# ifftshift of an 8192 x 8192 matrix in DRAM-to-DRAM copies: seven small copies go, half a block opens and closes the scalar queue, and the right half trails the left by 384 rows

## The chip, the core and the metric

The kernel runs on one core of one Trainium2 chip. It uses no compute engine for its work: two engines, SyncE and ScalarE, each issue copies from DRAM to DRAM into a queue of their own, and 16 DMA engines of the core serve both queues. The metric is the device time of one execution in microseconds (us).

## The reference

```python
def setup_inputs():
    return {
        "x": np.random.randn(8192, 8192).astype(np.float32),
    }

def reference(x: np.ndarray) -> np.ndarray:
    return np.fft.ifftshift(x)
```

Both sides are even, so the shift swaps the four quadrants: output row r, column c comes from input row (r + 4096) mod 8192, column (c + 4096) mod 8192. Nothing is computed. 268.4 MB are read once and written once.

## The kernel before

An output row is cut into a left half (columns 0 to 4095) and a right half (columns 4096 to 8191), 16 KiB each. The left halves of all 8192 rows go through the queue of SyncE (SP, `nc.sync`), the right halves through the queue of ScalarE (ACT, `nc.scalar`). The helper `copy` (line 26) issues one copy; it works out the source address from the destination row and column and uses the same pattern `dims` on both sides.

A **block** is 256 rows (`rows = ENGINES * per`, 16 times 16). Its pattern, `back` (line 45), has three levels: 16 neighbouring rows, then 16 steps of 16 rows *upwards*, then the 16 KiB of a row half. The outermost level is 16 wide, and the 16 DMA engines take one row of each group of 16. So a block gives every engine 16 packets of 16 KiB on that queue. I call one such set of 16 packets, one on each engine, a **round**: 16 row halves, 256 KiB, and a distance of 512 KiB in memory to the next round. A queue has 32 blocks, or 512 rounds.

Both queues go from the bottom of the matrix to its top. The loop of line 47 takes four blocks at a time. The left half takes them in the order 3, 2, 1, 0; the right half (line 50) takes block `(n + 2) % 4`, so 1, 0, 3, 2. While the left half is in block 3 or 2 of four, the right half is 512 rows above it, and while the left half is in 1 or 0, the right half is 512 rows below it.

Before the loop, lines 36 to 42 treat the first 16 rows of the right half on their own. Seven **small copies** on the scalar queue take them in four column strips of 4 KiB a row. Three strips are cut in two, after 14, 9 and 4 rows:

```python
    for n, k in enumerate((14, 9, 4)):
        col = hc + n * strip
        copy(nc.scalar, start + rows - ENGINES, col, [[C, k], [1, strip]])
        copy(nc.scalar, start + rows - ENGINES + k, col, [[C, ENGINES - k], [1, strip]])
```

A copy of k rows occupies k engines, so the engines get between one and seven small packets before the long copies. The block that those rows belong to is then issued with 15 steps in place of 16 (`rest`, line 46).

The order of the work is set by the two queues and by semaphores that the framework assigns in turn. There are eight of them for copies, and a copy whose semaphore was used before waits on its issuing engine until the earlier copy has landed. In the long run each queue has four blocks under way: a copy waits for the one four places ahead of it on its own queue. At the start it is different. The seven small copies and the first sync block take all eight semaphores. The second sync block therefore waits for the first sync block to land, and the first four long scalar copies wait for small copies.

Of the kernel before, what the change touches and what calls it, by code (L numbers as in the profile page):

```python
# [1 line left out]

# [4 lines left out]


ENGINES = 16


@with_exitstack
def kernel(
    ctx: ExitStack,
    tc: tile.TileContext,
    x: bass.AP,
    out: bass.AP,
):
    nc = tc.nc
    R, C = x.shape  # L20
    hr = R // 2
    hc = C // 2
    per = 16
    rows = ENGINES * per

    def copy(queue, row, col, dims):

        src = (row + hr) % R * C + (col + hc) % C
        queue.dma_start(
            out=bass.AP(out.tensor, out.offset + row * C + col, dims),  # L30
            in_=bass.AP(x.tensor, x.offset + src, dims),
        )

    start = R - 3 * rows
    strip = hc // 4
    for n, k in enumerate((14, 9, 4)):
        col = hc + n * strip
        copy(nc.scalar, start + rows - ENGINES, col, [[C, k], [1, strip]])  # L40
        copy(nc.scalar, start + rows - ENGINES + k, col, [[C, ENGINES - k], [1, strip]])
    copy(nc.scalar, start + rows - ENGINES, hc + 3 * strip, [[C, ENGINES], [1, strip]])


    back = [[C, ENGINES], [-ENGINES * C, per], [1, hc]]
    rest = [[C, ENGINES], [-ENGINES * C, per - 1], [1, hc]]
    for first in range(R - 4 * rows, -1, -4 * rows):
        for n in (3, 2, 1, 0):
            copy(nc.sync, first + n * rows + rows - ENGINES, 0, back)
            right = first + (n + 2) % 4 * rows  # L50
            if right == start:
                copy(nc.scalar, right + rows - 2 * ENGINES, hc, rest)
            else:
                copy(nc.scalar, right + rows - ENGINES, hc, back)


# [1 line left out]
_INS = ['x']  # L58
_OUTS = [((8192, 8192), 'float32')]


# [23 lines left out]
```

## Time and profile before

| | |
|---|---|
| median of 3 runs | 810.01 us (808.99 to 810.94) |
| profiled execution, its own time | 812.71 us |
| its span in the profile | 810.9 us |
| moved | 268.44 MB read, 268.44 MB written |
| mean rate | 331 GB/s each way, 662 GB/s read and written together |
| copies | 32 blocks on SP; 7 small ones, one of 15 steps and 31 blocks on ACT |
| share of the 16 DMA engines' time | SP's queue (q1) 49.7%, ACT's queue (q10) 49.6% |

The span is counted from the first instruction; 1.81 us of the execution's own time lie outside it. The four memsets on POOL are constants of the framework, 0.2 us in all. No compute engine has any other work, so the profile's parts on engines are nearly empty, and what is to be read is the part on DMA: the rate in slices of time, the packets, and when copies are issued and land. In answers about stretches of time each line gives the stretch, its length, POOL's busy time, a clock that is of no interest here, the mean busy share of the 16 DMA engines and the rate in GB/s. Packets are counted whole in these, so a short stretch can show a share a little over 1.

### The profile page before, as it was taken

What the parts mean: (1) busy time and instruction counts of PE and PEld (TensorE: products, weight loads), DVE (VectorE), ACT (ScalarE), POOL (GpSimd) and SP (SyncE); (2) the same over time, 40 slices, a digit from 0 to 9 for tenths busy, and PEclk for the clock granted to TensorE, in tenths of its full rate; (3) what the DMA queues carried; (4) which work ended last, traced back from release to release, by engine and by line L of the source; (5) the groups of instructions that cost most, each with busy time, mean ns of one, the idle gap of its engine ahead of it and who ended that gap; (6) DMA issues with size and microseconds to landing.
All of it is one profiled execution on the core that took longest, in us unless ns stands there. A gap on an engine that the chain in (4) does not pass through costs nothing. (4 is left out here: it accounts for less than half of the span.)

```text
span 810.9 us, 116 instructions
## 1 busy us (share of the span) xinstructions
POOL 0.2 (0%) x4
## 2 busy tenths in 40 slices
POOL 0000000000000000000000000000000000000000
DMA  9999999999999999999999999999999999999998
GB/s 302 328 335 329 334 333 331 331 335 330 326 331 329 331 335 330 332 332 337 335 336 333 333 337 330 334 335 331 336 331 333 335 334 335 333 330 336 333 338 296
DMA packets 17520, 268.44 MB, mean 331 GB/s; under 512 B 1088, under 2 KB 1088, under 8 KB 1152
## 3 DMA queue, kind: packets, MB, share of 16 engines
q1 hardware_dynamic: 8704, 134.22, 49.7%
q10 hardware_dynamic: 8816, 134.22, 49.6%
HBM read 268.44 MB, written 268.44 MB: 662 GB/s over the span
## 5 line engine op out<-in xcount | busy, mean ns | idle before, releaser
L69 POOL MEMSET const-bfloat16-1.0<- 128x1 bf16 x1 | 0.1, 102 | 0.0
L69 POOL MEMSET const-uint8-127<- 128x1 uint8 x1 | 0.1, 102 | 0.0
L69 POOL MEMSET const-float32-0.0<- 128x1 f32 x1 | 0.1, 99 | 0.2 <-issue 0.2
L69 POOL MEMSET const-float32-1.0<- 128x1 f32 x1 | 0.1, 99 | 0.0
## 6 DMA issues: line engine op xcount, KB each, us to landing
out_dram<-in_x_dram SPq DMA_DIRECT2D x32, 4096.0 KB, 100.9
out_dram<-in_x_dram ACTq DMA_DIRECT2D x31, 4096.0 KB
out_dram<-in_x_dram ACTq DMA_DIRECT2D x1, 3840.0 KB
out_dram<-in_x_dram ACTq DMA_DIRECT2D x1, 64.0 KB, 10.8
out_dram<-in_x_dram ACTq DMA_DIRECT2D x1, 56.0 KB
out_dram<-in_x_dram ACTq DMA_DIRECT2D x1, 48.0 KB
out_dram<-in_x_dram ACTq DMA_DIRECT2D x1, 36.0 KB
out_dram<-in_x_dram ACTq DMA_DIRECT2D x1, 28.0 KB
```

What stands on the lines that cost most here:

```text
L69: nc = _bacc.Bacc("TRN2", target_bir_lowering=False, num_devices=1)
```

## The change

The seven small copies and the 15-step copy go. The scalar queue now begins with half a block (8 steps, 128 rows), goes on with 31 whole blocks, and ends with another half. Its blocks therefore lie half a block off those of the sync queue. The scalar queue begins 384 rows above the bottom and goes straight upwards, wrapping around at the top, so the right half is written 384 rows further back than the left one throughout, where it was alternately 512 rows above and 512 below. Both orders of issue stay as they were otherwise, with four copies of each queue under way; since there are no small copies that take semaphores, all of the first four copies of each queue are issued without a wait.

```diff
-    start = R - 3 * rows
-    strip = hc // 4
-    for n, k in enumerate((14, 9, 4)):
-        col = hc + n * strip
-        copy(nc.scalar, start + rows - ENGINES, col, [[C, k], [1, strip]])
-        copy(nc.scalar, start + rows - ENGINES + k, col, [[C, ENGINES - k], [1, strip]])
-    copy(nc.scalar, start + rows - ENGINES, hc + 3 * strip, [[C, ENGINES], [1, strip]])
 
+    def back(queue, below, col, steps):
+        last = (below - 1) % R + 1 - ENGINES
+        copy(queue, last, col, [[C, ENGINES], [-ENGINES * C, steps], [1, hc]])
 
-    back = [[C, ENGINES], [-ENGINES * C, per], [1, hc]]
-    rest = [[C, ENGINES], [-ENGINES * C, per - 1], [1, hc]]
-    for first in range(R - 4 * rows, -1, -4 * rows):
-        for n in (3, 2, 1, 0):
-            copy(nc.sync, first + n * rows + rows - ENGINES, 0, back)
-            right = first + (n + 2) % 4 * rows
-            if right == start:
-                copy(nc.scalar, right + rows - 2 * ENGINES, hc, rest)
-            else:
-                copy(nc.scalar, right + rows - ENGINES, hc, back)
+    half = per // 2
+    start = R - rows - half * ENGINES
+    back(nc.scalar, start, hc, half)
+    below = start - half * ENGINES
+    for left in range(R, 0, -rows):
+        back(nc.sync, left, 0, per)
+        back(nc.scalar, below, hc, per if left > rows else half)
+        below -= rows
```

## The prediction

> **What bounds the kernel now.** I read the page's slices first, then the DMA queues, then the waits of the sync queue, then the rate in stretches of time that I chose from the landing times.
>
> The page and its DMA part:
>
> ```profile
> DMA  9999999999999999999999999999999999999998
> GB/s 302 328 335 329 334 333 331 331 335 330 326 331 329 331 335 330 332 332 337 335 336 333 333 337 330 334 335 331 336 331 333 335 334 335 333 330 336 333 338 296
> DMA packets 17520, 268.44 MB, mean 331 GB/s; under 512 B 1088, under 2 KB 1088, under 8 KB 1152
> q1 hardware_dynamic: 8704, 134.22, 49.7%
> q10 hardware_dynamic: 8816, 134.22, 49.6%
> ```
>
> The 16 DMA engines are busy in every slice, and the two queues' packets fill 99.3% of their time. So nothing waits to be issued for long; the time is the number of packets on an engine times the length of a packet. An engine has 1024 packets of 16 KiB. In the trace's packet records these last 786 ns on average, but a third of them last 608 to 611 ns and one in seven over 1000 ns. The floor of 611 ns would be 16 engines x 16,384 B / 611 ns = 429 GB/s; the rest is packets that get in each other's way in the memory. **The length of a packet is what a change must move.** Only the first and the last slice are low.
>
> The waits of the sync queue:
>
> ```profile
> SPq L29 <- DMA out_dram<-in_x_dram: 686.8, 28, 28.4
> ```
>
> 28 of 32 sync blocks waited for an older block to land. With three more blocks queued behind it (25.2 us each) that costs nothing, except for the first such wait, at the head. The head and the tail in stretches:
>
> ```profile
> 0.00:2.00 2.00, 0.20 (x4) 1.00 0.00 0
> 2.00:5.00 3.00, 0.00 (x0) 1.00 0.97 350
> 5.00:7.00 2.00, 0.00 (x0) 1.00 1.07 373
> 7.00:16.00 9.00, 0.00 (x0) 1.00 1.00 321
> ...
> 18.00:20.00 2.00, 0.00 (x0) 1.00 1.08 352
> 20.00:22.00 2.00, 0.00 (x0) 1.00 0.90 270
> 22.00:30.00 8.00, 0.00 (x0) 1.00 1.01 338
> 30.00:805.00 775.00, 0.00 (x0) 1.00 1.00 333
> 805.00:808.00 3.00, 0.00 (x0) 1.00 1.01 339
> 808.00:810.00 2.00, 0.00 (x0) 1.00 0.28 98
> ```
>
> Until about 13 us SP is almost alone (the small copies are a few packets), from 18 to 22 us ACT is alone (SP's second block waited for its first, landed at 19.25 us), and from 805 us ACT is alone again. One queue alone gets 321 to 373 GB/s, both together 333: **a second stream adds no rate and, at this distance, takes none**. Only the dip at 20 to 22 us shows engines idle.
>
> Last, a sync block from one landing to the next, in eighths (two rounds each):
>
> ```profile
> 379.40:382.53 3.13, 0.00 (x0) 1.00 1.04 351
> 382.53:385.66 3.13, 0.00 (x0) 1.00 0.97 340
> 385.66:388.78 3.12, 0.00 (x0) 1.00 0.97 326
> 388.78:391.91 3.13, 0.00 (x0) 1.00 0.99 330
> 391.91:395.04 3.13, 0.00 (x0) 1.00 1.04 345
> 395.04:398.17 3.13, 0.00 (x0) 1.00 0.98 325
> 398.17:401.29 3.12, 0.00 (x0) 1.00 1.00 326
> 401.29:404.42 3.13, 0.00 (x0) 1.00 0.98 330
> ```
>
> The means of the eighths over 26 such blocks are 339, 343, 326, 327 and 338, 331, 327, 328 GB/s (standard error 2.5). The rate depends on where in memory the streams stand, and repeats about every half block, 8 rounds or 4 MiB. That is a sign of conflicts by address.
>
> **The change part by part.**
>
> *Small copies out.* 64 packets of 4 KiB last 159 ns each at the floor, 64 x 159 / 16 = 0.64 us of every engine's time, and 64 closing packets of 9 ns in place of none make 0.04 us. They become 16 packets of 16 KiB, 16 x 786 / 16 = 0.79 us. Sum +0.11 us. ACT spends 0.57 to 1.42 us on each issue, from 0.73 to 6.5 us, while SP's first block keeps the engines full, so ACT's issue time and the 10.8 us to the landing of the last small copy are covered and their end is worth nothing. The row says that 4 KiB in 159 ns is as fast as 16 KiB in 611.
>
> The Trainium skill's page "DMA: Bandwidth & Descriptors", section "Bandwidth", has it otherwise: transfers under 64 KB are descriptor-dominated, 64 KB in 0.95 us. By it, as an estimate, seven small copies of about 0.95 us would cost 6.6 us where bulk takes 0.8, and the change would end at 804. The trace speaks against this: they run beside another queue's packets.
>
> *Waits at the head.* SP's second to fourth and ACT's first four blocks no longer wait. The dip goes: 2 us x (333 - 270) / 333 = 0.4 us gained. At most the 321 GB/s of 7 to 16 us rises to 333 as well, 0.3 us more; at least, eight issues in a row make a dip of their own and nothing is gained. I take -0.4, since the dip is the one place with idle engines. The start stays: the first packet comes at 2.18 us, behind SP's first issue (0.73 to 1.38 us).
>
> *Tail.* SP's blocks now lead ACT's by what they gain at the start. In the packet records ACT's first packet comes 2.9 us after its issue, behind four packets that each engine had taken from SP. So I expect a lead of 4 to 5.5 rounds, as now (4.4 to 5.9), and ACT alone for the last 4.5 us, as now (SP's last packet ends at 805.2, ACT's at 809.7). Cost 0, with +-0.9 for the engines' ends, which now spread from 808.3 to 809.7.
>
> *The half-block phase.* A copy's closing packet takes its queue's turn on each engine. The records show it: two packets of one queue in a row come some 18 times per block on 16 engines, on either queue, at the other's boundaries. So SP's lead drops by one round when an SP block ends and rises when an ACT block ends. Now the low lead lasts from an SP landing to the next ACT landing, 8.5 of 25.2 us; with the half block it lasts 8 rounds longer, some 21 us. Over 26 blocks the low-lead stretch ran at 338.5 GB/s and the other at 329.2. Most of this is the address pattern above: set against the same place half a block later, the low lead is ahead by 1, 11 and -1 GB/s in its three eighths (the third counts for 0.7), +4 +- 2.5. Ends: nothing, or +4 GB/s over another half block, +0.65% of 806 us, -5.2 us. I take nothing, since the parity of the half block in memory explains the difference as well.
>
> *The distance.* 512 rows, above or below, become 384 above. Without the lead that is 32 rounds either way before and 24 after: the same multiple of 8 rounds, so the half-block pattern should stay, but 4 MiB of relative position are new. The old two distances differ by just 1024 rows, 32 MiB, so that their equal rates (block means 331.6 to 333.1 by place in the group of four) say nothing of 24. Bounds: the better and the worse stretch. 338.5 throughout is 806 x (1 - 332.3 / 338.5) = -14.8 us; the worst slice of the page, 326, is +15.6 us. I take zero, because one stream alone is no faster than two.
>
> *Sum.* 0.1 - 0.4 + 0 + 0 + 0 = -0.3 us, against the profiled execution's 812.71 us (span 810.9 and 1.81 outside): 812.4. That execution lies 2.7 us above the median; against 810.01 the forecast is 809.7.
>
> **The rivals.**
>
> *Slower: the new distance collides.* One mechanism: at 24 rounds left and right packets meet in the same part of memory more often. For it: the rate does depend on address, by 327 to 343 GB/s within a block. Against: two streams lose nothing against one. Price: the second stretch's 329.2 throughout is 806 x (332.3 / 329.2 - 1) = +7.6, so 817.5; 326 is 825.5. It decides from 0.2%, a mean under 331.6 GB/s.
>
> *Faster: the low lead is worth its 4 GB/s*, 804.5; 802.3 if the whole difference of the stretches swaps with their lengths ((16.7 x 338.5 + 8.5 x 329.2) / 25.2 = 335.4). Against: three eighths, two of them with no difference.
>
> *Engines in step.* The small packets, one to seven on an engine, set the engines apart. Without them they may run in step for longer. In the records the only rounds in step, the first four, ran mostly at the floor of 611 ns until the first small packet at 5.03 us. At 393 GB/s (3 to 5 us by the stretches) for 15 us more this gains 15 x (393 - 333) / 393 = 2.3 us, 807.5. Against: from 7 to 16 us the engines were within 0.5 us of their mean and got 321.
>
> The Trainium skill's same page, section "Latency and other measured facts", says that streams in lock-step at a power-of-two row pitch lose up to half the rate and that 4 KiB of padding restores it. By it engines in step would be slower, and as an estimate 12 MiB is no better a distance than 16. The first rounds here speak against harm from being in step, and no run here shows another pitch.
>
> **How the numbers follow.** Rate as before, head and tail alone: 809.7, own range 807.5 to 811.8, chance 0.42. Slower by the distance, 812 to 826: 0.33. Faster, by the lead or in step or a luckier distance, 799 to 808: 0.25. Faster and slower by less than 0.2% (808.4 to 811.6, about what measurement tells from no change) are the same: of the first case 0.20 falls there, 0.12 below and 0.10 above. Faster 0.37, same 0.20, slower 0.43. Leaving out a tenth at each end gives 801 to 821.
>
> **What would show it.** Right: no stretch before 30 us with a share near 0.90 but the first 2 us; both queues' shares within 0.2 of 49.7 and 49.6; slices at 331 to 335; SP done 4 to 5 us before the end, low lead for 20 us of 25. Wrong: slices shifted as a whole, 327 and lower (the distance) or 336 and higher (the lead), or a first slice near 330 (in step), or one queue far ahead and a tail of more than 8 us.

## The result and the profile after

The kernel after takes 814.52 us (median of 19 runs, 809.67 to 819.71), the kernel before beside it 811.07 (808.99 to 812.49). The ratio is 1.0046, 95% interval 1.0030 to 1.0062: slower by about half a per cent, by more than the 0.2% that I called the same. Its runs also lie further apart: their standard deviation is 2.8 us, that of the kernel before 0.9. The profiled execution of after took 816.82 us, 815.0 of them span; it is one of the slower ones.

The page after, parts on slices and DMA queues:

```profile
DMA  8999999999999999999999999999999999999998
GB/s 303 334 332 334 330 335 334 336 330 333 335 330 326 333 329 335 338 322 337 333 329 326 332 324 326 330 335 327 331 328 328 328 333 335 333 330 334 330 328 289
DMA packets 17424, 268.44 MB, mean 329 GB/s; under 512 B 1040, under 2 KB 1040, under 8 KB 1040
...
q10 hardware_dynamic: 8720, 134.22, 49.6%
q1 hardware_dynamic: 8704, 134.22, 49.4%
```

The small packets are gone (1040 closing packets are left of 1152 packets under 8 KB). The two queues' shares add up to 99.0%, where they were 99.3. The first half of the slices is as it was; from the 18th slice on many lie under 330.

The waits of the sync queue after:

```profile
SPq L29 <- DMA out_dram<-in_x_dram: 691.0, 28, 25.4
```

The same 28 waits. The longest is now a block's time, 25.4 us; before it was 28.4, the one that ended at 50.3 us, after the late start of SP's second block.

The same kernel in stretches of time (stretch, length, POOL, clock, share of the DMA engines, GB/s), first the head and the tail:

```profile
2.00:5.00 3.00, 0.00 (x0) 1.00 0.98 350
5.00:7.00 2.00, 0.00 (x0) 1.00 1.06 352
7.00:16.00 9.00, 0.00 (x0) 1.00 1.01 335
16.00:18.00 2.00, 0.00 (x0) 1.00 0.91 303
18.00:20.00 2.00, 0.00 (x0) 1.00 1.06 360
20.00:22.00 2.00, 0.00 (x0) 1.00 0.93 311
...
809.00:812.00 3.00, 0.00 (x0) 1.00 0.98 328
812.00:814.00 2.00, 0.00 (x0) 1.00 0.26 82
```

and then the whole span in five pieces, after:

```profile
0.00:30.00 30.00, 0.20 (x4) 1.00 0.94 318
30.00:410.00 380.00, 0.00 (x0) 1.00 0.99 332
410.00:530.00 120.00, 0.00 (x0) 1.00 1.00 328
530.00:784.00 254.00, 0.00 (x0) 1.00 0.99 331
784.00:815.00 31.00, 0.00 (x0) 1.00 0.91 303
```

and before:

```profile
0.00:30.00 30.00, 0.20 (x4) 1.00 0.94 310
30.00:410.00 380.00, 0.00 (x0) 1.00 1.00 332
410.00:530.00 120.00, 0.00 (x0) 1.00 1.00 334
530.00:780.00 250.00, 0.00 (x0) 1.00 1.00 334
780.00:811.00 31.00, 0.00 (x0) 1.00 0.92 311
```

The head gained: 318 against 310 GB/s over 30 us is 0.7 us. Up to 410 us the two are level. The loss lies in the second half, where 328 and 331 stand against 334: 120 x (334 / 328 - 1) + 254 x (334 / 331 - 1) = 4.5 us.

What kind of loss it is, the packet records tell. If each engine's packets are summed and the sum is taken from the span, the rest is time in which an engine had no packet. All packets of 16 KiB last 786.5 ns on average before and 786.8 after: over the whole span the packets did not get longer. But between 5 us and the last 8 us an engine had no packet for 0.7 us before and for 4.3 us after. So 3.7 of the 4.1 us that this execution's span is longer are **gaps between packets**, with blocks queued behind them all the time.

The gaps do not all lie where the rate fell, though. From 30 to 410 us they cost an engine 1.9 us more than before, and packets that are 5 ns shorter (784.8 ns against 789.8) make up for it. From 410 to 780 us they cost 1.4 us more, and packets that are 6 ns longer (789.4 against 783.6) cost the larger part, some 2.7 us. The length of the packets wanders within one execution as much as the gaps do, and the two means agree because these differences cancel.

The packets can be put together into chains, one for each engine, by the end of one and the start of the next. Between 25 and 800 us the gaps of all engines, each counted by itself, then sum to 124 us, where they are 67 us in the trace of before. (Successive records also overlap by up to 5 ns, which the time without a packet above has taken off.) 105 of the 124 us lie in four of the 16 rounds of an SP block, counted from 0: the rounds 1, 6, 9 and 14. Since 9 is 1 + 8 and 14 is 6 + 8, that is twice the same two places, 4 MiB apart.

### The profile page after: what moved, and what is told of

It is laid out like the page before. It is cut to its first block, busy times and chain, and to the rows that moved or that the text cites. A ratio compares the mean times of both kernels' runs of the same rounds, so it can differ in the third digit from the quotient of the medians.

```text
span 815.0 us, 110 instructions
## 1 busy us (share of the span) xinstructions
POOL 0.2 (0%) x4
## 2 busy tenths in 40 slices
DMA packets 17424, 268.44 MB, mean 329 GB/s; under 512 B 1040, under 2 KB 1040, under 8 KB 1040
```

## The experiments

Every kernel was measured beside the kernel before, in 12 runs (10 in one case). The level of the kernel before turned out to differ by job: about 811 us in three of eight and 822 us in five. Nothing in a kernel explains that, nor does the chip alone: two of the chips served two jobs each, and each had one job of either level. In an 822 us job the packets of the kernel after last 794.2 ns on average in place of 787, so that everything is 1% longer. The results are therefore set against this level; all ratios are to the kernel before in the same job. Further on I speak of 811 jobs and 822 jobs.

### The first job: four variants, an 822 job

My theories were three. One: the distance that the streams really keep, the nominal one less SP's lead, counts modulo 8 rounds; from the trace of after I read a lead of 2.2 to 3.7 rounds in place of 4.4 to 5.9. (That was one round too few: by the packet records SP is 3.2 to 4.7 rounds ahead in the kernel after.) Two: the small copies set the engines apart and that is worth something. Three: the half-block phase costs.

The kernel before without small copies (whole blocks, 512 rows):

```diff
-    start = R - 3 * rows
-    strip = hc // 4
-    for n, k in enumerate((14, 9, 4)):
...
-            if right == start:
-                copy(nc.scalar, right + rows - 2 * ENGINES, hc, rest)
-            else:
-                copy(nc.scalar, right + rows - ENGINES, hc, back)
+            copy(nc.scalar, right + rows - ENGINES, hc, back)
```

> The kernel before without its small copies: whole blocks, right half alternately 512 rows above and below, all of the first four copies of each queue issued at once. Before 811.1 us, after 814.5. Theory 1, the distance that the streams really keep (nominal distance minus SP's lead, modulo 8 rounds or 4 MiB): SP's lead falls from 5 rounds to 2.5 as in the kernel after, so 29.5 rounds, the remainder of the kernel after; 814.5, +0.4%. Theory 2, the small copies set the engines apart and that is worth something: they are gone; 814.5. Theory 3, the half-block phase of the copies' ends: it isn't there; 811.

The kernel after with the small copies put back in its first 16 right rows:

```diff
+    strip = hc // 4
+    for n, k in enumerate((14, 9, 4)):
+        col = hc + n * strip
+        copy(nc.scalar, start - ENGINES, col, [[C, k], [1, strip]])
+        copy(nc.scalar, start - ENGINES + k, col, [[C, ENGINES - k], [1, strip]])
+    copy(nc.scalar, start - ENGINES, hc + 3 * strip, [[C, ENGINES], [1, strip]])
-    back(nc.scalar, start, hc, half)
...
         back(nc.sync, left, 0, per)
+        if left == R:
+            back(nc.scalar, start - ENGINES, hc, half - 1)
```

> The kernel after with the seven small copies for the first 16 rows of the right half: half block, distance 384, SP's second block waiting for its first as before. Theory 1: the wait at the head brings the lead back to 5 rounds, 19 rounds between the streams, remainder 3 as before; 811. Theory 2: engines set apart as before; 811. Theory 3: the half-block phase is there; 814.5.

The kernel after with another distance, 480 rows here and 352 in a second kernel. A scalar block that would cross row 4096 or the top is cut in two there:

```diff
     def back(queue, below, col, steps):
-        last = (below - 1) % R + 1 - ENGINES
-        copy(queue, last, col, [[C, ENGINES], [-ENGINES * C, steps], [1, hc]])
+        while steps:
+            below = (below - 1) % R + 1
+            n = min(steps, ((below - 1) % hr + 1) // ENGINES)
+            copy(queue, below - ENGINES, col, [[C, ENGINES], [-ENGINES * C, n], [1, hc]])
+            below -= n * ENGINES
+            steps -= n
...
-    start = R - rows - half * ENGINES
+    start = R - 480
```

> The kernel after with 480 rows in place of 384, two scalar blocks cut in two where a row wraps. With a lead of 2.6 rounds the streams stand 27.4 rounds apart, as in the kernel before (27). Theory 1: 811. Theories 2 and 3: 814.5.

> The kernel after with 352 rows in place of 384: 19.4 rounds between the streams, the remainder modulo 8 of the kernel before and a total that is 8 rounds off. Theory 1 modulo 8: 811. If the whole distance counts and not the remainder: near 814. Theories 2 and 3: 814.5.

Measured, with the kernel before at 822.44 us (35 runs):

| kernel | median us | ratio | 95% interval | standard deviation us |
|---|---|---|---|---|
| before without small copies | 822.84 | 1.0000 | 0.9985 to 1.0015 | 2.0 |
| after with small copies | 822.69 | 1.0006 | 0.9995 to 1.0018 | 1.1 |
| distance 480 | 822.39 | 1.0001 | 0.9985 to 1.0017 | 1.9 |
| distance 352 | 822.74 | 1.0003 | 0.9988 to 1.0017 | 2.0 |

All are level, so none of the three theories is told from another. The kernel after with small copies is level although SP's lead in its profile is 13 to 14 rounds, not the 5 that I expected. Leads from 2.4 to 14 rounds and distances from 352 to 512 rows make no difference of 0.2% here. Theory one was not tested as I meant it: the remainders that 480 and 352 rows were to hit are worked out from the lead that I had misread, and the lead in those two traces is 3.3 to 5.4 rounds.

### The second job: the kernel after itself, an 811 job

> The kernel after, unchanged, beside the kernel before. Theory A, the change costs 0.4% by its access pattern whatever the chip: ratio 1.003 to 1.006. Theory B, what the change costs depends on where the two matrices lie and on the chip, and on a chip where the kernel before takes 822 us every variant costs the same: ratio 0.999 to 1.001 where the kernel before takes 822 us, 1.003 to 1.006 where it takes 811 us.

> The kernel before without its small copies, a second time. If the kernel after is slower beside it here: theory 1 (distance kept, remainder of 8 rounds) and theory 2 (small copies) expect +0.4%, theory 3 (half-block phase) expects no change. If the kernel after is level with the kernel before here, this one is level too.

> The kernel after with 480 rows in place of 384, a second time. If the kernel after is slower beside it here: theory 1 expects no change against the kernel before, theories 2 and 3 expect +0.4%. Otherwise level.

Measured, with the kernel before at 811.55 us (29 runs, standard deviation 1.4):

| kernel | median us | ratio | 95% interval | standard deviation us |
|---|---|---|---|---|
| after | 815.48 | 1.0041 | 1.0019 to 1.0064 | 3.0 |
| before without small copies | 813.80 | 1.0015 | 0.9996 to 1.0035 | 2.3 |
| distance 480 | 812.68 | 1.0014 | 0.9995 to 1.0033 | 2.1 |

The 0.4% is there again. The two others lie between the kernel before and the kernel after and can't be told from the kernel before. No theory expected 1.0015 of both.

The profiled execution of the kernel after fell on one of its fastest runs here, 810.1 us. So there are two profiles of the same instructions, 815.0 and 808.3 us long. The page of the short one:

```profile
GB/s 305 334 335 334 334 335 335 337 330 336 332 335 337 330 334 334 333 331 338 329 336 333 337 330 339 331 337 334 334 331 332 336 331 332 332 333 335 335 333 295
...
q1 hardware_dynamic: 8704, 134.22, 50.3%
q10 hardware_dynamic: 8720, 134.22, 49.1%
```

There is no low second half, and the shares add up to 99.4% in place of 99.0. By the packet records the mean packet is 783.4 ns (786.8 in the long one), 3.5 us over 1024 packets, and the time without a packet between 5 us and the last 8 us is 1.2 us (4.3). The gaps don't cluster in the rounds 1, 6, 9 and 14 (11 of 75 us). So the kernel after *can* run faster than the median of the kernel before, and what costs is something that comes and goes between executions of the same program.

### Three more jobs for the parts, all 822 jobs

I now wanted to tell the parts in an 811 job: small copies of unequal number, equal small copies, distance and phase. The kernel before with equal small copies keeps the waits at the head, but gives every engine seven packets (in its traces SP leads by 7 to 9 rounds, not by the 5 that I expected):

```diff
-    strip = hc // 4
-    for n, k in enumerate((14, 9, 4)):
-        col = hc + n * strip
-        copy(nc.scalar, start + rows - ENGINES, col, [[C, k], [1, strip]])
-        copy(nc.scalar, start + rows - ENGINES + k, col, [[C, ENGINES - k], [1, strip]])
-    copy(nc.scalar, start + rows - ENGINES, hc + 3 * strip, [[C, ENGINES], [1, strip]])
+    strip = hc // 8
+    for n in range(6):
+        copy(nc.scalar, start + rows - ENGINES, hc + n * strip, [[C, ENGINES], [1, strip]])
+    copy(nc.scalar, start + rows - ENGINES, hc + 6 * strip, [[C, ENGINES], [1, 2 * strip]])
```

The two others are the kernel after with `start = R - 512`, and whole blocks at 384 rows:

```diff
-    half = per // 2
-    start = R - rows - half * ENGINES
-    back(nc.scalar, start, hc, half)
-    below = start - half * ENGINES
+    below = R - 384
     for left in range(R, 0, -rows):
         back(nc.sync, left, 0, per)
-        back(nc.scalar, below, hc, per if left > rows else half)
+        back(nc.scalar, below, hc, per)
         below -= rows
```

> The kernel after with the seven unequal small copies put back for the first 16 rows of its right half; the waits at the head come back with them. On a chip where the kernel before takes 811 us: if the small copies, or the waits that they bring, are what the kernel after lacks, level with the kernel before (0.999 to 1.001) and its runs within some 4 us of each other; if the distance of 384 rows or the half-block phase costs, 1.002 to 1.004. Where the kernel before takes 822 us: level.

> The kernel before with seven small copies that give each engine the same number of packets (six of 2 KiB and one of 4 KiB per row); waits at the head and SP's lead of 5 rounds stay. If it is the unequal number that sets the engines apart: about 1.002, and runs spread over 7 us or more as in the kernels without small copies. If it is the waits at the head and the lead: level, spread as before.

> The kernel after with 512 rows in place of 384: half-block phase and no small copies, but the distance of the kernel before. If the half-block phase costs, as in the kernel after, 1.004. If the distance of 384 costs, 1.0015 as the kernel before without small copies.

> Whole blocks on both queues, no small copies, right half 384 rows back (scalar blocks cut where a row wraps). If the distance costs: 1.004 as the kernel after. If the half-block phase costs: 1.0015 as the kernel before without small copies.

> The kernel after, a third time. Where the kernel before takes 811 us: 1.004. Where it takes 822 us: theory B (the cost hangs on the placing of the session) expects level, theory A 1.004.

> The kernel after with the seven unequal small copies and their waits at the head. Where the kernel before takes 811 us: level if the change's cost is the lack of small copies or waits, 1.004 if it is the distance or the half-block phase. Where it takes 822 us: level, as twice before.

> The kernel before with seven equal small copies. Where the kernel before takes 811 us: level if the waits at the head and the lead that follows matter, 1.002 if it is the unequal number of packets on the engines. Where it takes 822 us: level, as once before.

> Whole blocks, no small copies, 384 rows. Where the kernel before takes 811 us: 1.004 if the distance costs beside the lack of small copies, 1.0015 if the half-block phase does. Where it takes 822 us: level, as once before.

The third job had the kernel before at 821.67 us (35 runs), the fourth at 822.04 (35 runs):

| kernel, job | median us | ratio | 95% interval | standard deviation us |
|---|---|---|---|---|
| after with small copies, third | 822.04 | 1.0008 | 0.9996 to 1.0020 | 1.4 |
| equal small copies, third | 821.73 | 0.9997 | 0.9981 to 1.0012 | 1.2 |
| distance 512, third | 823.60 | 1.0025 | 1.0009 to 1.0041 | 1.9 |
| whole blocks, 384 rows, third | 822.45 | 1.0007 | 0.9994 to 1.0021 | 1.5 |
| **after**, fourth | 822.82 | 1.0006 | 0.9992 to 1.0021 | 1.2 |
| after with small copies, fourth | 822.35 | 1.0008 | 0.9995 to 1.0020 | 1.4 |
| equal small copies, fourth | 821.57 | 0.9997 | 0.9986 to 1.0008 | 1.1 |
| whole blocks, 384 rows, fourth | 822.34 | 1.0007 | 0.9993 to 1.0021 | 1.7 |

The kernel after itself is level in an 822 job. That is what theory B (the cost hangs on the job) expected and theory A (a cost of the access pattern everywhere) did not. Equal small copies are level with the unequal ones of the kernel before, in 24 runs; the unequal number of packets is worth nothing here.

Twice more I measured the kernel after with small copies alone, for the chance of an 811 job:

> The kernel after with the seven unequal small copies and their waits at the head, once more, for a session in which the kernel before takes 811 us. There: level if the change's cost is the lack of the small copies or of the waits, 1.004 if it is the distance or the half-block phase. Where the kernel before takes 822 us: level, as three times before.

> As the run before: the kernel after with the small copies and their waits. Where the kernel before takes 811 us: level if the lack of small copies or waits is the cost, 1.004 if the distance or the half-block phase is. Where it takes 822 us: level.

Both were 822 jobs: 822.13 against 822.12 (1.0003, 0.9991 to 1.0014), and 823.73 against 821.69 (1.0031, 1.0018 to 1.0043; 10 runs). One kernel thus has ratios of 1.0006, 1.0008, 1.0008, 1.0003 and 1.0031 in five jobs. The last interval shuts out the other four values. The interval of one job holds for that job; between jobs a ratio moves by some 0.2% more.

### One stream alone

The last run takes the second stream away: all 64 blocks on the sync queue, the left half of all rows and then the right half.

```diff
-    half = per // 2
-    start = R - rows - half * ENGINES
-    back(nc.scalar, start, hc, half)
...
+    for col in (0, hc):
+        for below in range(R, 0, -rows):
+            back(nc.sync, below, col, per)
```

> All 64 blocks on the sync queue, no small copies: the left half of all rows, then the right half. There is one stream, so no distance, no lead and no half-block phase between two. If packets get in each other's way among the 16 engines of one stream, as the head and tail of the kernel before suggest (321 to 373 GB/s alone, 333 together): within 0.5% of the kernel before. If the two streams' meeting is what lengthens packets: faster by several per cent, towards the 429 GB/s of the floor. If an engine needs the second queue to go on without a gap: slower, shares of the DMA engines well under 99%.

It was an 811 job: 816.92 us against 811.06, ratio 1.0052 (1.0026 to 1.0079). Its standard deviation is 2.8 us without one run of 825.8 us that stands apart. Its page and two stretches:

```profile
GB/s 292 319 324 327 325 324 330 323 325 337 327 331 331 337 332 327 334 332 334 331 330 342 334 328 339 332 331 339 334 335 332 330 334 330 338 334 329 337 333 289
...
q1 hardware_dynamic: 17408, 268.44, 99.2%
```

```profile
30.00:400.00 370.00, 0.00 (x0) 1.00 1.00 329
400.00:805.00 405.00, 0.00 (x0) 1.00 1.00 333
```

One queue keeps the engines as busy as two. Its packets last 789.4 ns on average, against a floor of 611 that a third of them reach, as before. So two streams' meeting is not needed to lengthen packets. That the engines' packets lengthen one another, the ends of all 20 traces show, where one engine after the other runs out of work. I took the last 64 packets of 16 KiB of each trace: the 86 that had on average fewer than six packets under way at once, their own included, last 615 ns on average, and the 1025 with twelve or more 792 ns. Where on the way the packets hold each other up, no run here shows.

The 0.5% lies just outside the band that I had called level. It is as large as the cost of the kernel after, in a kernel that has no distance, no lead, no phase and no small copies.

## Why the prediction was wrong

I forecast 809.7 us, level with the kernel before, and it is 0.46% slower. The time lies in the range from 801 to 821, and slower had the largest chance, 0.43; the likeliest single case, 0.42, was the wrong one.

**The small copies.** I costed their removal at +0.1 us in packets and nothing in ACT's issue time. As a cost of the copies themselves nothing contradicts that: the kernel before without them is at 1.0000 in an 822 job and 1.0015 (0.9996 to 1.0035) in an 811 job. Put back into the kernel after, they are within 0.1% of the kernel before in four jobs of five, but these were 822 jobs, where the kernel after itself is level. The estimate from the Trainium skill's page "DMA: Bandwidth & Descriptors", section "Bandwidth", by which seven small copies would cost 6.6 us, is not borne out: the kernels without them are no faster. That section's figures are for loads into SBUF, the core's own memory, issued from GpSimd, not for copies from DRAM to DRAM beside a busy queue.

**The head.** The size was about right, the reason was not: -0.4 forecast, -0.7 at most, 0.7 us measured over 30 us in the long execution (312 against 310 GB/s, 0.2 us, in the short one). I had read the dip of before at 20 to 22 us, share 0.90, as idle engines. The packet records show an engine without a packet for less than 0.01 us there; the 16 KiB packets that start in it are long, 873 ns on average, and a stretch counts a packet whole where it starts. So there was no idle time to win back. Shares of 0.91 and 0.93 stand in the long execution of after as well, at 16 to 18 and 20 to 22 us. The gain came from 7 to 16 us, 335 in place of 321 GB/s (324 in the short one), the step that I had put at the end of the range.

**The tail and the lead.** I expected a lead of 4 to 5.5 rounds; it is 3.2 to 4.7. ACT's first packet does come behind four SP packets, at 5.1 us, but between 5 and 7 us ACT then started 27 packets and SP 16, so that the lead fell by 0.7 of a round at once. The tail is 3.5 us of ACT alone (810.5 to 813.9) in place of 4.5 and costs the same: in the last 8 us an engine is without a packet for 2.1 us, before for 2.0.

**The half-block phase.** It works as described: the stretch of low lead grew from 8.5 to 19.0 us of 25.4. I took nothing for it because the place in memory explained the difference as well, and for the lead that was right: over 26 blocks the low-lead stretch of after ran at 330.9 GB/s and the other at 332.2, in the short execution at 334.2 and 333.0. The advantage of 9 GB/s that the stretches of before showed was none of the lead's. Whether the phase costs in another way is not shown.

**The distance.** I took 0, and a cost is neither shown nor shut out. 352, 384 and 480 rows are level in 822 jobs, and one stream with no distance at all is as slow as the kernel after, so that a distance is not needed for such a cost. In the one 811 job that has two distances, 480 rows lie at 1.0014 (0.9995 to 1.0033) and 384 rows at 1.0041; the medians are 2.8 us apart, but the runs overlap (809.5 to 816.4 and 810.1 to 819.1). That one stream is no faster than two was right. 512 rows with the half-block phase lie at 1.0025 in an 822 job, hardly more than the 0.2% by which ratios differ between jobs. The rival "the new distance collides" named the right side, but its mark is not there: slices shifted as a whole. Up to 410 us the rate is 332 GB/s in both, and the packets last 786.8 ns against 786.5. (Its prices, 817.5 and 825.5, stand 0.2 us above what their terms add to 809.7; nothing hangs on that.)

**Engines in step.** At the head they did run closer together: the closing packets of SP's first block spread over 1.5 us (1.1 in the short execution), before over 3.0. It brought no rate near 393 GB/s, and my sign for it was weak: of the first 64 packets of before, 27 were at the floor (613 ns or less), not most. Over the whole run they were not closer, 1.97 us a block on average against 1.69. So the gain that I priced did not come. The loss by the Trainium skill's same page, section "Latency and other measured facts", did not come at the head either, where closer engines got more and not less; that page calls its mechanism an inference.

**The step that failed** is the sum's "rate as before; head and tail alone", with its range of 807.5 to 811.8: for the middle of the run I put phase and distance at nothing, and nothing for the small copies and waits beyond the head. The head gave 0.2 to 0.7 us and the tail cost nothing, yet the kernel after is 3.5 and 3.9 us slower in two 811 jobs, so that the middle costs about 4 us. My reason for zero, that one stream is no faster than two, speaks of the length of packets and not of time without a packet. I also took the middle as fixed by the access pattern, from one execution of the kernel before, whose runs happened to lie close together. The runs showed a middle that differs between executions of the same program by 6.7 us (815.0 and 808.3 us of span), of which 3.1 us were gaps and 3.5 longer packets. The kernel before is steadier and its middle better in 811 jobs; the kernel after has 0.4% more, the one-queue kernel 0.5%. In the one 822 job that has the kernel after, the difference is gone.

**What stays open.** Which of the change's parts costs the 0.4% is not settled, and the gaps are not shown to be it. The 4.3 us are the most in any of the 20 traces and the 0.7 us of before the least; the four other traces of 811 jobs have 1.2 to 1.6 us, the short one of the kernel after among them. In 811 jobs four kernels were measured beside the kernel before, and none of them has its small copies with the waits at the head: 1.0041 to 1.0046 (after, twice), 1.0015 (before without small copies), 1.0014 (480 rows) and 1.0052 (one queue). In 822 jobs their runs spread a little more than those of kernels with small copies (1.2 to 2.0 us against 1.1 to 1.4; before 0.8 to 1.5). That makes the small copies or their waits a suspect, though not by the gaps: in the traces of 822 jobs an engine is without a packet for 1.2 to 3.0 us in kernels with small copies and for 0.9 to 2.5 us in those without. What would show it, the kernel after with small copies in an 811 job, is missing: all five jobs that had it were 822 jobs. Equal small copies, which were level, and whole blocks at 384 rows were measured in 822 jobs alone as well. Why an engine goes without a packet for a few tenths of a us at the same places of a block, and what sets the level of a job, no run here tells.

## What to carry to other kernels

Where all DMA engines are busy throughout, the time of one profiled execution is one draw: look at the spread of the runs, and split span into packet time and time without a packet before saying that packets got longer. A difference between two stretches of a periodic kernel must first be compared with the same place of the next period; here that turned a lever of 7 us into nothing. For half a per cent, repeat the comparison in several jobs: an interval from one job does not cover the next.

## What the runs showed that I had not expected

- One queue of copies from DRAM to DRAM keeps the 16 engines as busy as two: 99.2% of the span against 99.3%, 329 GB/s each way against 331 before.
- The same kernel takes 811 us in some jobs and 822 in others, steady within a job. Packets are longer throughout (783 to 787 ns against 794 for the kernel after), and the share at the floor of 611 ns stays at a third.
- The packet that closes a copy on an engine, 4 bytes and 9 ns, takes its queue's turn: at the boundary of a block on one queue the other gets two packets in a row, on each engine. So SP's lead moves by one round at each such boundary, in the kernel after between about 3.5 and 4.5.
